# Row stages by single tiles: one 512-wide matmul for both token parts, and VectorE sums the halves

## The chip, the cores and the metric

The kernel runs on one core of a Trainium2 chip. Its metric is the device time of one execution in microseconds (us): the median of three runs before the change is 413.46 us. Five engines work side by side, each through its own queue in order: PE (TensorE) does matmuls, with the loads of its stationary operand shown apart as PEld; DVE (VectorE) and ACT (ScalarE) do elementwise work; POOL (GpSimd) does little here; SP (SyncE) issues the transfers. PE writes its results to PSUM, of which one accumulator tile here is 128 x 512 fp32, one bank; DVE and ACT read PSUM and work in SBUF.

## What is computed

One decoder layer of width 1024 on 256 tokens (two token tiles, t = 0 and 1) with a memory of 256 tokens. In the reference, cut short:

```python
h = rms_norm(x, g_pre_mix);  proj = h @ w_in        # MoBA attention and RetNet retention on proj
x = x + rms_norm(concat(mo, ro) @ w_out, g_post_mix)
q = rms_norm(x, g_pre_cross) @ w_cq                 # cross-attention, 4 heads of 256
k, v = split(rms_norm(mem, g_mem) @ w_ckv)
x = x + rms_norm(softmax(q k^T / 16) v @ w_co, g_post_cross)
gu = rms_norm(x, g_pre_ffn) @ w_gate_up             # d_ff = 2816 = 22 tiles of 128
x = x + rms_norm((silu(gu[:, :2816]) * gu[:, 2816:]) @ w_down, g_post_ffn)
```

All of it is fp32. The norms' row scales commute with the products: the kernel multiplies by the gain ahead of a matmul and by the inverse root mean square behind it.

## The kernel before, in words

**Three products for one.** Each fp32 operand is split in two parts of a faster format (fp32r): the high part is a rounded copy, the low part is what is left. A product is then three matmuls, high x high, high x low and low x high (helper `tri` and the loops of the three kinds of steps).

**Weights.** All weights lie in DRAM as 130 blocks of 128 x 1024 fp32 in the order of use. `load_weight` fetches a block (ring of 5 raw tiles), `split_weight` (L128 on) makes its two parts: the high one by ACT (L133), the low one by DVE (L134), in a ring of 9 tiles `hl`.

**Steps.** The whole program is a list of steps that is walked once, so PE's order is the list's. There are three kinds. A *col* step multiplies a token tile (stationary) by 512 weight columns (moving): six matmuls of 512 columns. A *down* step does the same for the last FFN product. A *row* step turns this round: the weights are stationary, 128 columns of them at a time, and the 256 tokens are moving, so that the result comes out transposed, as the next stage needs it. Row steps make the cross keys (k stage, `memT`), the cross queries (cq stage, `x1T`) and the gate and up products (`x2T`) apart from their first 512 columns.

A row block is 256 rows (two k tiles) by 512 columns (four tiles of 128 outputs). It feeds two steps, one for each pair of output tiles. A step is 12 matmuls of 256 columns: for two output tiles and two k tiles, high weights by high tokens (L868), the same weights by low tokens (L870), low weights by high tokens (L871). An accumulator holds the pair, 2 x 256 columns, and is finished after four blocks. Two accumulators are open at once.

**Stages.** In order: input projection (24 blocks, col), output projection (8, col), k (8, row), cq (8, row), cross values (8, col), cross output (8, col), first FFN chunk (8, col), then four gate/up stages (4 gate and 4 up blocks each, row) with a down stage (4 blocks) behind each, a last gate/up stage of two tiles (4 blocks) and the last 6 down blocks.

**Side work.** What DVE and ACT do besides the splits is written as generators. When a step finishes an accumulator, its `done` function does the work at once or spawns a generator; `yield n` lets it rest for n steps. The table `WAIT` holds these numbers by name. At the end of each step the due generators go on, then at most one weight block is split: if its ring place is free, if the pace allows it, and if no generator went on in this step or fewer than seven blocks are ahead (`low` 6). All engines follow the order in which this walk writes their instructions.

What becomes of a finished pair: `k_done` multiplies by the row of memory scales (`row_bcast`, DVE), copies the high part (ACT) and subtracts for the low part (DVE). `cq_done` splits straight from PSUM. `ffn_gate_T` multiplies by the row of scales (L511, DVE), takes Silu (L512, ACT), multiplies by the row again (L514, DVE). `ffn_up_T` multiplies the up accumulator by that (L520, DVE) and splits the product into `fT` (L524 ACT, L525 DVE), which the down steps read.

`post_and_pre` stands between stages: `post_add` adds the normed branch to x (L411), then ACT squares x for the next norm (L151), and after a wait `xw` PE transposes x; ACT and DVE scale it by the gains and split it into `x1T` or `x2T` (L427, L430), in two halves with a wait `xh` between them. The k stage is the time in which `x1T` is made; the cq stage reads it. `row_rms` makes the row of scales.

PSUM has four tiles of tag S (`accS`), three of tag B (`accB`) and one of tag C (`accC`).

Of the kernel before, what the change touches and what calls it, by code (L numbers as in the profile page):

```python
# [14 lines left out]
P = 128  # L15
# [7 lines left out]
NQ = 130  # L23

WAIT = {
# [7 lines left out]
}  # L33
WARM = 8

# [6 lines left out]
def tile_hybrid_layer(  # L42
# [127 lines left out]
    def row_rms(key):  # L170
# [3 lines left out]
        for t in range(2):  # L174
            nc.tensor.transpose(c[:, t, :], rstd[f"{key}{t}"][:, 0:1].to_broadcast([P, P]), ident)
        nc.scalar.activation(T[f"R_{key}"], c[:, 0:2, :].rearrange("p t k -> p (t k)"), AF.Copy)

    def row_bcast(key):
        return T[f"R_{key}"][:, None, :].to_broadcast([P, 2, 256])


    active = []
# [223 lines left out]
    def post_add(stage, t):  # L406
        ss, cg = posts.pop(f"{stage}{t}")
        r = inv_rms(f"p_{stage}{t}", ss[:, 0:1], ss[:, 1:2])
        for half in range(2):
            xs = x_sb[:, t, half * 512:(half + 1) * 512]  # L410
            nc.vector.scalar_tensor_tensor(xs, cg[half], r[:, 0:1], xs, op0=ALU.mult, op1=ALU.add)  # L411

    def post_and_pre(stage, t, g, dst_name, key):
        post_add(stage, t)
        ss = small(f"ssx_{stage}{t}")
        mean_square(ss[:, 0:1], x_sb[:, t, :], D)
        inv_rms(f"{key}{t}", ss[:, 0:1])
        yield WAIT[f"xw_{stage}{t}"]
        dst = T[dst_name]
        for half in range(2):  # L420
            a = accS(f"xt_{stage}{t}{half}")
            for j in range(4):
                k = half * 4 + j
                nc.tensor.transpose(a[:, j * P:(j + 1) * P], x_sb[:, t, k * P:(k + 1) * P], ident)
            for j in range(4):
                k = half * 4 + j
                nc.scalar.activation(dst[:, 0, k, tok(t)], a[:, j * P:(j + 1) * P], AF.Copy, scale=gp[:, g, k:k + 1])  # L427
            for j in range(4):
                k = half * 4 + j
                nc.vector.scalar_tensor_tensor(dst[:, 1, k, tok(t)], a[:, j * P:(j + 1) * P], gp[:, g, k:k + 1],  # L430
                                               dst[:, 0, k, tok(t)].bitcast(F32), op0=ALU.mult, op1=ALU.subtract)
                emitted.add((dst_name, k, t))
            if half == 0:
                yield WAIT[f"xh_{stage}{t}"]
        if stage == "cross" and t == 1:
            yield WAIT["xrow"]
            row_rms("x2")
# [66 lines left out]
        nc.scalar.activation(sg, acc, AF.Silu, scale=rstd[f"x2{t}"][:, 0:1])  # L504
        T[f"sg0_{t}"] = sg

    def ffn_gate_T(j, pair, acc):
        sg = tmp2k(f"sg{j}_{pair}")
        T[f"sg{j}_{pair}"] = sg
        s3 = sg.rearrange("p (j m) -> p j m", j=2)  # L510
        nc.vector.tensor_tensor(out=s3, in0=acc.rearrange("p (j m) -> p j m", j=2), in1=row_bcast("x2"), op=ALU.mult)  # L511
        nc.scalar.activation(sg, sg, AF.Silu)  # L512
        yield WAIT[f"sr{pair}"] if j < 5 else 0
        nc.vector.tensor_tensor(out=s3, in0=s3, in1=row_bcast("x2"), op=ALU.mult)  # L514
        emitted.add(f"sg{j}_{pair}")

    def ffn_up_T(j, pair, acc):
        need(f"sg{j}_{pair if j < 5 else 0}")
        f = tmp2k(f"f{j}_{pair}")
        nc.vector.tensor_tensor(out=f, in0=acc, in1=T[f"sg{j}_{pair}"], op=ALU.mult)  # L520
        k = 2 * pair if j < 5 else 0
        hi = T["fT"][:, j % 2, 0, k:k + 2, :].rearrange("p j m -> p (j m)")
        lo = T["fT"][:, j % 2, 1, k:k + 2, :].rearrange("p j m -> p (j m)")
        nc.scalar.activation(hi, f, AF.Copy)  # L524
        nc.vector.tensor_tensor(out=lo, in0=f, in1=hi.bitcast(F32), op=ALU.subtract)  # L525
        emitted.update(("fT", 4 * j + i, t) for i in (k, k + 1) for t in range(2))

    def final(t, half):
        nc.sync.dma_start(out[tok(t), half * 512:(half + 1) * 512], x_sb[:, t, half * 512:(half + 1) * 512])
# [30 lines left out]
            if t == 1:  # L560
                spawn(load_gpost(1, WAIT["gp1"]))

    def k_done(c, pair, acc):
        k = 4 * c + 2 * pair
        kf = tmp2k(f"kf{k}").rearrange("p (j m) -> p j m", j=2)
        nc.vector.tensor_tensor(out=kf, in0=acc.rearrange("p (j m) -> p j m", j=2), in1=row_bcast("mem"), op=ALU.mult)
        hi_lo(T["ckh"][:, k:k + 2, :], T["ckl"][:, k:k + 2, :], kf)

    def cq_done(c, pair, acc):
        k = 4 * c + 2 * pair  # L570
        hi_lo(T["cqh"][:, k:k + 2, :], T["cql"][c][:, 2 * pair:2 * pair + 2, :],
              acc.rearrange("p (j m) -> p j m", j=2))
        if k == 6:
            for t in range(2):
                spawn(cross_unit(t), WAIT[f"cu{t}"])

# [51 lines left out]
                continue  # L628
            steps.append(("col", base + i, t, st, kp, (c, t), s == 0, s + 1 == count[c], done))

    def row_steps(order, done, st):


        for c, kp in order:
            for pair in range(2):
                steps.append(("row", nq[0], pair, st, kp, (c, pair), kp == 0, kp == 3, done))
            nq[0] += 1

    def plain(chunks):
# [20 lines left out]
    for c in range(2):  # L660
        col_steps([(c, kp) for kp in (2, 3, 0, 1)], both, out_done, "mixT")
    mark("k")
    row_steps(plain([0, 1]), k_done, "memT")
    mark("cq")
    row_steps(plain([0, 1]), cq_done, "x1T")
    mark("v")
    col_steps(plain([0, 1]), both, v_done, "memT")
    mark("co")
# [6 lines left out]
        else:  # L675
            spawn(ffn_up(t, acc))

    def gu_done(c, pair, acc):
        j, up = c % 100, c >= 100
        if up:  # L680
            ffn_up_T(j, pair, acc)
        elif j == 5 and pair == 1:
            T["sg5_1"] = T["sg5_0"]
            ffn_up_T(j, pair, acc)
        else:
            spawn(ffn_gate_T(j, pair, acc))

    def down_steps(js, tiles):
        blocks = [(j, kk) for j in js for kk in range(4 if j < 5 else 2)]
# [6 lines left out]

    col_steps(plain([0, 1]), first_then, gu_first, "x2T")
    for j in range(1, 5):
        row_steps(plain([j]), gu_done, "x2T")
        row_steps(plain([100 + j]), gu_done, "x2T")  # L700
        if j < 4:
            down_steps([j - 1], both)
    down_steps([3], both)
    row_steps(plain([5]), gu_done, "x2T")
    down_steps([4, 5], [(0,)])
    blocks_base = nq[0] - 6
    for half in range(2):
# [100 lines left out]
    for i, s in enumerate(steps):  # L808
# [28 lines left out]
        elif s[0] == "col":  # L837
            _, q, t, st, kp, key, first, last, done = s
            if first:
                accs[key] = accB(f"acc{i}")  # L840
            acc = accs[key]
            h = hls[q].rearrange("p s (k n) -> p s k n", k=2)
            for kk in range(2):
# [8 lines left out]
                del accs[key]  # L852
                done(key[0], t, acc)
        elif s[0] == "row":
            _, q, pair, st, kp, key, first, last, done = s
            if first:
                accs[key] = accS(f"acc{i}") if st != "x2T" and key[0] == 1 else accB(f"acc{i}")
            acc = accs[key]
            h = hls[q].rearrange("p s (k n) -> p s k n", k=2)
            for b in range(2):  # L860
                dst = acc[:, b * 256:(b + 1) * 256]
                n = slice((2 * pair + b) * P, (2 * pair + b + 1) * P)
                for kk in range(2):
                    k = 2 * kp + kk
                    need((st, k, 0), (st, k, 1))
                    xh = T[st][:, 0, k, :]
                    xl = T[st][:, 1, k, :]
                    nc.tensor.matmul(dst, h[:, 0, kk, n], xh, start=(first and b == 0 and kk == 0), stop=False,  # L868
                                     skip_group_check=True)
                    nc.tensor.matmul(dst, h[:, 0, kk, n], xl, start=False, stop=False, skip_group_check=True)  # L870
                    nc.tensor.matmul(dst, h[:, 1, kk, n], xh, start=False, stop=(last and kk == 1),  # L871
                                     skip_group_check=True)
            if last:
                del accs[key]
                done(key[0], pair, acc)
        elif s[0] == "down":
            _, q, t, j, kk, halves = s
            for half in halves:
# [34 lines left out]
def _layout(inputs):  # L913
# [15 lines left out]
        blocks += cols(w_in, c * 512, k4)  # L929
    for c in range(2):  # L930
        blocks += cols(w_out, c * 512, (2, 3, 0, 1))
    w_cq, w_ckv, w_co = a["w_cq"][0], a["w_ckv"][0], a["w_co"][0]
    for w, cs in ((w_ckv, (0, 1)), (w_cq, (0, 1)), (w_ckv, (2, 3))):
        for c in cs:
            blocks += cols(w, c * 512, k4)
    for half in range(2):
        for c in range(2):
            blocks += cols(w_co, c * 512, (2 * half, 2 * half + 1))
# [3 lines left out]
    def down(j):  # L942
        return [dn[k * P:(k + 1) * P] for k in range(4 * j, min(4 * j + 4, ff // P))]

    for j in range(5):
        blocks += cols(gu, j * 512, k4) + cols(gu, ff + j * 512, k4)
        if 1 <= j < 4:
            blocks += down(j - 1)
    blocks += down(3)
    last = np.concatenate([gu[:, 2560:2816], gu[:, ff + 2560:ff + 2816]], axis=1)  # L950
    blocks += cols(last, 0, k4) + down(4) + down(5)
    weights = np.stack(blocks)

    def tiles_T(v):
# [54 lines left out]
```

## Time and profile before

| | us |
|---|---|
| median of three runs (413.32 to 413.69) | 413.46 |
| the profiled execution's own time | 413.18 |
| its span in the profile | 411.4 |
| DVE, splits of weights (L134, 132 operations) | 154.0 |
| ACT, splits of weights (L133, 132 operations) | 131.7 |
| gate/up stage (192 row matmuls), 275.44 to 298.48 | 23.04 |
| down stage (48 matmuls), 298.48 to 309.38 | 10.90 |

The profile is of one execution. Times of instructions are given from the span's start. Matmuls are pipelined: one is shown for longer than it holds PE up, and what it costs is the distance of its start to the next one's. Idle time of an engine stands with what ended it.

### The profile page before, as it was taken

How to read it: one execution, taken by the hardware profiler on the slowest of the kernel's cores; microseconds unless marked ns; L12 is line 12 of the kernel's file. 1: busy time of each engine (PE TensorE's matmuls, PEld its weight loads, DVE VectorE, ACT ScalarE, POOL GpSimd, SP SyncE). 2: the span in 40 equal slices, each digit the busy share in tenths (PEclk: the TensorE clock that was granted, in tenths of full speed). 3: DMA queues.
4: the chain of work that ended last, by engine and by line, in shares of the span. 5: the costliest groups of instructions: out<-in, count | busy, mean ns of one | idle time of the engine just before them, and what ended most of it. 6: DMA issues, size and time to landing. Idle time of an engine off the chain costs nothing.

```text
span 411.4 us, 6399 instructions
## 1 busy us (share of the span) xinstructions
PE 404.0 (98%) x2530; PEld 358.6 (87%) x2530; DVE 260.5 (63%) x356; ACT 219.0 (53%) x360; POOL 11.0 (3%) x21
## 2 busy tenths in 40 slices
PE   8999999999999999999999999999999999999994
PEld 4888787878899999888888899989989989998983
DVE  5876975866858884485367687664674764566332
ACT  5887686746656662584266666352453553444111
POOL 0010100000010000000011000000000000000000
PEclk9999999999999999999999999999999999999998
DMA  8998754475727674225414867676546447353001
GB/s 292 408 348 276 242 188 151 138 255 187 229 80 252 210 261 169 81 68 189 155 51 155 289 226 253 206 231 180 189 150 227 150 146 266 106 202 104 0 27 77
DMA packets 21630, 76.23 MB, mean 185 GB/s; under 512 B 2400, under 2 KB 2656, under 8 KB 21600
## 3 DMA queue, kind: packets, MB, share of 16 engines
q1 hardware_dynamic: 21456, 75.56, 54.3%
q8 instruction: 20, 0.33, 0.3%
q10 hardware_dynamic: 144, 0.26, 0.2%
q14 instruction: 10, 0.08, 0.1%
HBM read 74.76 MB, written 1.05 MB: 184 GB/s over the span
## 4 chain that ended last, share of the span: by engine, by line
PE 95%; issue 2%; DMA 1%; ACT 1%; DVE 0%; SPq 0%; DVEq 0%; POOLq 0%; POOL 0%
PE acc L871 12%; PE acc L868 12%; PE acc L870 12%; PE acc L848 12%; PE acc L850 12%; PE acc L849 12%; PE down L890 4%; PE down L892 4%; PE down L891 4%; PE acc L835 2%; DMA xr<-in_gx_dram 1%; PE s_m L276 1%; PE o_m L305 1%; PE pt_m L255 1%; PE ro L358 0%
## 5 line engine op out<-in xcount | busy, mean ns | idle before, releaser
L134 DVE TENSOR_TENSOR hl<-raw,hl 128x1024 fp32r<-128x1024 f32 (+1 forms) x132 | 154.0, 1197 | 49.6 <-ACT hl L133 49.4
L133 ACT ACTIVATE hl<-raw 128x1024 fp32r<-128x1024 f32 (+1 forms) x132 | 131.7, 1036 | 42.0 <-PE acc L871 15.0
L868 PE MATMUL acc<-x2T,hl 128*128 128x256 f32 x288 | 81.8, 284 | 0.0
L871 PE MATMUL acc<-x2T,hl 128*128 128x256 f32 x288 | 81.6, 283 | 0.0
L870 PE MATMUL acc<-x2T,hl 128*128 128x256 f32 x288 | 81.6, 283 | 0.0
L870 PEld LDWEIGHTS acc<-x2T,hl 128*128 128x128 f32 x288 | 55.3, 192 | 0.2
L868 PEld LDWEIGHTS acc<-x2T,hl 128*128 128x128 f32 x288 | 55.3, 192 | 0.2
L871 PEld LDWEIGHTS acc<-x2T,hl 128*128 128x128 f32 x288 | 55.3, 192 | 0.0
L890 PE MATMUL down<-hl,fT 128*128 128x512 f32 x88 | 34.3, 390 | 0.0
L891 PE MATMUL down<-hl,fT 128*128 128x512 f32 x88 | 34.3, 390 | 0.0
L892 PE MATMUL down<-hl,fT 128*128 128x512 f32 x88 | 34.3, 389 | 0.0
L848 PE MATMUL acc<-hl,xT 128*128 128x512 f32 x80 | 32.7, 409 | 0.0
L850 PE MATMUL acc<-hl,xT 128*128 128x512 f32 x80 | 31.3, 392 | 0.0
L849 PE MATMUL acc<-hl,xT 128*128 128x512 f32 x80 | 31.2, 390 | 0.0
L892 PEld LDWEIGHTS down<-hl,fT 128*128 128x128 f32 x88 | 16.5, 188 | 3.5
L890 PEld LDWEIGHTS down<-hl,fT 128*128 128x128 f32 x88 | 16.6, 188 | 3.3
L891 PEld LDWEIGHTS down<-hl,fT 128*128 128x128 f32 x88 | 16.6, 188 | 3.3
L512 ACT ACTIVATE sg<-sg 128x512 f32<-128x512 f32 x9 | 5.7, 632 | 24.9 <-DVE sg L511 24.9
L868 PE MATMUL acc<-memT,hl 128*128 128x256 f32 x64 | 18.4, 287 | 0.0
L870 PE MATMUL acc<-x1T,hl 128*128 128x256 f32 x64 | 18.1, 283 | 0.0
L871 PE MATMUL acc<-memT,hl 128*128 128x256 f32 x64 | 18.1, 283 | 0.0
L868 PE MATMUL acc<-x1T,hl 128*128 128x256 f32 x64 | 18.1, 283 | 0.0
(207 smaller groups left out, 727.8 us busy)
## 6 DMA issues: line engine op xcount, KB each, us to landing
raw<-in_weights_dram SPq DMA_DIRECT2D x129, 512.0 KB, 4.6
gpost<-in_gpost_dram SPq DMA_DIRECT2D x3, 512.0 KB, 6.0
x_sb<-in_x_dram SPq DMA_DIRECT2D x2, 512.0 KB, 6.9
memn<-in_mem_dram SPq DMA_DIRECT2D x2, 512.0 KB, 7.1
mr<-in_memT_dram SPq DMA_DIRECT2D x2, 512.0 KB, 5.2
out_dram<-x_sb SPq DMA_DIRECT2D x4, 256.0 KB, 2.0
xr<-in_gx_dram SPq DMA_DIRECT2D x1, 512.0 KB, 7.8
cst<-in_consts_dram SPq DMA_DIRECT2D x1, 512.0 KB, 8.6
```

The source lines that it names most:

```text
L133: nc.scalar.activation(h[:, 0, n], raw[:, n], AF.Copy)
L134: nc.vector.tensor_tensor(out=h[:, 1, n], in0=raw[:, n], in1=h[:, 0, n].bitcast(F32), op=ALU.subtract)
L835: nc.tensor.matmul(accs[(c, t)], T["xT"][:, hx, 2 * kp + kk, tok(t)], h[:, hw, :], start=begin, stop=False)
L848: nc.tensor.matmul(acc, xh, h[:, 0, kk, :], start=(first and kk == 0), stop=False)
L849: nc.tensor.matmul(acc, xh, h[:, 1, kk, :], start=False, stop=False)
L850: nc.tensor.matmul(acc, xl, h[:, 0, kk, :], start=False, stop=(last and kk == 1))
L868: nc.tensor.matmul(dst, h[:, 0, kk, n], xh, start=(first and b == 0 and kk == 0), stop=False, skip_group_check=True)
L870: nc.tensor.matmul(dst, h[:, 0, kk, n], xl, start=False, stop=False, skip_group_check=True)
L871: nc.tensor.matmul(dst, h[:, 1, kk, n], xh, start=False, stop=(last and kk == 1), skip_group_check=True)
L890: nc.tensor.matmul(acc, fh, wh, start=first, stop=False, skip_group_check=True)
L891: nc.tensor.matmul(acc, fh, wl, start=False, stop=False, skip_group_check=True)
L892: nc.tensor.matmul(acc, fl, wh, start=False, stop=last, skip_group_check=True)
```

## The change

The blocks of the row stages are cut otherwise. A block is now all eight k tiles of one output tile (8 x 128 columns), so one block makes one output tile, in two steps of four k tiles each. For each k tile two matmuls are issued: the high weights by both token parts, high and low, in one matmul of 512 columns, whose result fills both halves of the bank; and the low weights by the high token part, 256 columns, added to the first half. At the end the sum is first half plus second half: ACT copies the second half to SBUF, DVE adds the first from PSUM. The multiplications and splits behind it work on 256 columns, one tile at a time, and each is spawned as a generator with waits of its own. Gate and up tiles alternate. The order of the weight blocks in DRAM follows; the number of blocks stays 130.

```diff
-            _, q, pair, st, kp, key, first, last, done = s
...
-                for kk in range(2):
-                    k = 2 * kp + kk
-                    nc.tensor.matmul(dst, h[:, 0, kk, n], xh, ...)
-                    nc.tensor.matmul(dst, h[:, 0, kk, n], xl, ...)
-                    nc.tensor.matmul(dst, h[:, 1, kk, n], xh, ...)
+            _, q, half, st, nt, done = s
+            if half == 0:
+                accs["row"] = accB(f"acc{i}")
+            acc = accs["row"]
+            for k in range(4 * half, 4 * half + 4):
+                need((st, k, 0), (st, k, 1))
+                n = slice(k * P, (k + 1) * P)
+                nc.tensor.matmul(acc.rearrange("p (s m) -> p s m", s=2), hls[q][:, 0, n], T[st][:, :, k, :],
+                                 start=(k == 0), stop=False, skip_group_check=True)
+                nc.tensor.matmul(acc[:, 0:256], hls[q][:, 1, n], T[st][:, 0, k, :], start=False, stop=(k == 7),
+                                 skip_group_check=True)
+            if half == 1:
+                spawn(done(nt, acc))
...
+    def ffn_gate_T(i, acc):
+        buf = tmp2k(f"sg{i}")
+        T[f"sg{i}"] = buf
+        sg = buf[:, 0:256]
+        nc.scalar.activation(sg, acc[:, 256:512], AF.Copy)
+        yield WAIT["g_add"]
+        nc.vector.tensor_tensor(out=sg, in0=acc[:, 0:256], in1=sg, op=ALU.add)
+        nc.vector.tensor_tensor(out=sg, in0=sg, in1=T["R_x2"], op=ALU.mult)
+        yield WAIT["g_silu"]
         nc.scalar.activation(sg, sg, AF.Silu)
+        yield WAIT["g_row"]
+        nc.vector.tensor_tensor(out=sg, in0=sg, in1=T["R_x2"], op=ALU.mult)
+    def ffn_up_T(i, acc):
+        buf = T.pop(f"sg{i}")
+        f = buf[:, 256:512]
+        nc.scalar.activation(f, acc[:, 256:512], AF.Copy)
+        yield WAIT["u_add"]
+        nc.vector.tensor_tensor(out=f, in0=acc[:, 0:256], in1=f, op=ALU.add)
+        nc.vector.tensor_tensor(out=f, in0=f, in1=buf[:, 0:256], op=ALU.mult)
+        yield WAIT["u_hl"]
+        hi_lo(T["fT"][:, (i // 4) % 2, 0, i % 4, :], T["fT"][:, (i // 4) % 2, 1, i % 4, :], f)
...
+    def k_done(i, acc):
+        kf = tmp2k(f"kf{i}")[:, 0:256]
+        nc.scalar.activation(kf, acc[:, 256:512], AF.Copy)
+        yield WAIT["k_add"]
+        nc.vector.tensor_tensor(out=kf, in0=acc[:, 0:256], in1=kf, op=ALU.add)
+        nc.vector.tensor_tensor(out=kf, in0=kf, in1=T["R_mem"], op=ALU.mult)
+        yield WAIT["k_hl"]
+        hi_lo(T["ckh"][:, i, :], T["ckl"][:, i, :], kf)
...
     def post_and_pre(stage, t, g, dst_name, key):
         post_add(stage, t)
+        yield WAIT[f"xa_{stage}{t}"]
...
-                accs[key] = accB(f"acc{i}")
+                accs[key] = accC(f"acc{i}").rearrange("p j k -> p (j k)") if st == "memT" and key == (1, 0) else accB(f"acc{i}")
```

`cq_done` is cut to one tile in the same way as `k_done`, without the multiplication. New waits: g_add, u_add, k_add and q_hl 0, g_silu and g_row 1, u_hl and k_hl 2; xa_mix0 3, xa_mix1 5, xa_cross 2 each. Changed ones: xw_mix0 4 to 2, xw_mix1 9 to 5, xw_cross0 7 to 5, xw_cross1 3 to 2, xrow 1 to 3, nm_c1 3 to 5, cpv0 6 to 7. In DRAM, a gate/up stage's blocks are gate tile, up tile, gate tile, and so on.

More of the change, by code (lines that the diff above doesn't have):

```diff
@@ L176, in row_rms @@
         nc.scalar.activation(T[f"R_{key}"], c[:, 0:2, :].rearrange("p t k -> p (t k)"), AF.Copy)
-    def row_bcast(key):
-        return T[f"R_{key}"][:, None, :].to_broadcast([P, 2, 256])
     active = []
@@ L505, in ffn_gate @@
         T[f"sg0_{t}"] = sg
[L507 to L526, printed above, removed]
+    def ffn_gate_T(i, acc):
[7 more added lines that the diff above has]
+        yield WAIT["g_silu"]
+        nc.scalar.activation(sg, sg, AF.Silu)
+        yield WAIT["g_row"]
+        nc.vector.tensor_tensor(out=sg, in0=sg, in1=T["R_x2"], op=ALU.mult)
+        emitted.add(f"sg{i}")
+    def ffn_up_T(i, acc):
[3 more added lines that the diff above has]
+        yield WAIT["u_add"]
+        need(f"sg{i}")
+        nc.vector.tensor_tensor(out=f, in0=acc[:, 0:256], in1=f, op=ALU.add)
+        nc.vector.tensor_tensor(out=f, in0=f, in1=buf[:, 0:256], op=ALU.mult)
+        yield WAIT["u_hl"]
+        hi_lo(T["fT"][:, (i // 4) % 2, 0, i % 4, :], T["fT"][:, (i // 4) % 2, 1, i % 4, :], f)
+        emitted.update(("fT", i, t) for t in range(2))
     def final(t, half):
@@ L561, in out_done, with cq_done @@
                 spawn(load_gpost(1, WAIT["gp1"]))
[L563 to L573, printed above, removed]
+    def k_done(i, acc):
[6 more added lines that the diff above has]
+        hi_lo(T["ckh"][:, i, :], T["ckl"][:, i, :], kf)
+    def cq_done(i, acc):
+        qf = tmp2k(f"qf{i}")[:, 0:256]
+        nc.scalar.activation(qf, acc[:, 256:512], AF.Copy)
+        yield WAIT["k_add"]
+        nc.vector.tensor_tensor(out=qf, in0=acc[:, 0:256], in1=qf, op=ALU.add)
+        yield WAIT["k_hl"] if i < 7 else WAIT["q_hl"]
+        hi_lo(T["cqh"][:, i, :], T["cql"][i // 4][:, i % 4, :], qf)
+        emitted.add(f"cq{i}")
+        if i == 7:
+            need(*[f"cq{k}" for k in range(8)])
             for t in range(2):
@@ L629, in col_steps, with row_steps @@
             steps.append(("col", base + i, t, st, kp, (c, t), s == 0, s + 1 == count[c], done))
[L631 to L636, printed above, removed]
+    def row_steps(tiles, done, st):
+        for i in tiles:
+            for half in range(2):
+                steps.append(("row", nq[0], half, st, i, done))
             nq[0] += 1
@@ L662, in tile_hybrid_layer @@
     mark("k")
-    row_steps(plain([0, 1]), k_done, "memT")
+    row_steps(range(8), k_done, "memT")
     mark("cq")
-    row_steps(plain([0, 1]), cq_done, "x1T")
+    row_steps(range(8), cq_done, "x1T")
     mark("v")
@@ L676, in gu_first, with gu_done, gu_steps @@
             spawn(ffn_up(t, acc))
[L678 to L686, printed above, removed]
+    def gu_done(i, acc):
+        return ffn_up_T(i - 100, acc) if i >= 100 else ffn_gate_T(i, acc)
+    def gu_steps(tiles):
+        row_steps([i + up for i in tiles for up in (0, 100)], gu_done, "x2T")
     def down_steps(js, tiles):
@@ L698, in tile_hybrid_layer @@
     for j in range(1, 5):
-        row_steps(plain([j]), gu_done, "x2T")
-        row_steps(plain([100 + j]), gu_done, "x2T")
+        gu_steps(range(4 * j, 4 * j + 4))
         if j < 4:
@@ L703, in tile_hybrid_layer @@
     down_steps([3], both)
-    row_steps(plain([5]), gu_done, "x2T")
+    gu_steps((20, 21))
     down_steps([4, 5], [(0,)])
@@ L854, in tile_hybrid_layer @@
         elif s[0] == "row":
-            _, q, pair, st, kp, key, first, last, done = s
[L856 to L862, printed above, removed]
-                for kk in range(2):
-                    k = 2 * kp + kk
[L865 to L875, printed above, removed]
+            _, q, half, st, nt, done = s
[11 more added lines that the diff above has]
+                spawn(done(nt, acc))
         elif s[0] == "down":
@@ L931, in _layout, with rows @@
         blocks += cols(w_out, c * 512, (2, 3, 0, 1))
+    def rows(w, i):
+        return [w[:, i * P:(i + 1) * P].reshape(8, P, P).transpose(1, 0, 2).reshape(P, D)]
     w_cq, w_ckv, w_co = a["w_cq"][0], a["w_ckv"][0], a["w_co"][0]
-    for w, cs in ((w_ckv, (0, 1)), (w_cq, (0, 1)), (w_ckv, (2, 3))):
-        for c in cs:
-            blocks += cols(w, c * 512, k4)
+    for w in (w_ckv, w_cq):
+        for i in range(8):
+            blocks += rows(w, i)
+    for c in (2, 3):
+        blocks += cols(w_ckv, c * 512, k4)
     for half in range(2):
@@ L943, in down, with gate_up @@
         return [dn[k * P:(k + 1) * P] for k in range(4 * j, min(4 * j + 4, ff // P))]
-    for j in range(5):
-        blocks += cols(gu, j * 512, k4) + cols(gu, ff + j * 512, k4)
-        if 1 <= j < 4:
+    def gate_up(tiles):
+        return [b for i in tiles for b in rows(gu, i) + rows(gu, ff // P + i)]
+    blocks += cols(gu, 0, k4) + cols(gu, ff, k4)
+    for j in range(1, 5):
+        blocks += gate_up(range(4 * j, 4 * j + 4))
+        if j < 4:
             blocks += down(j - 1)
-    blocks += down(3)
-    last = np.concatenate([gu[:, 2560:2816], gu[:, ff + 2560:ff + 2816]], axis=1)
-    blocks += cols(last, 0, k4) + down(4) + down(5)
+    blocks += down(3) + gate_up((20, 21)) + down(4) + down(5)
     weights = np.stack(blocks)
```

15 rows, old and new, of the table WAIT are left out of this document.

## The prediction

> **What bounds the kernel now.** I read the busy times of the page first, then its chain of work that ended last, then the waits of PE:
>
> ```profile
> PE 404.0 (98%) x2530; PEld 358.6 (87%) x2530; DVE 260.5 (63%) x356; ACT 219.0 (53%) x360; POOL 11.0 (3%) x21
> ...
> PE 95%; issue 2%; DMA 1%; ACT 1%; DVE 0%; SPq 0%; DVEq 0%; POOLq 0%; POOL 0%
> ```
>
> ```profile
> PE warm L723 <- DVE junk L716: 1.2, 1, 1.2
> ```
>
> PE is busy for 404.0 of the span of 411.4 us, the chain is 95% PE, and PE's waits have one entry, 1.2 us ahead of the warm-up. So after the opening PE never waits for another engine, and the time is the sum of PE's pitches (start of one matmul to start of the next). An edit counts if it changes that sum, or if it makes PE wait. DVE and ACT have room on the mean, not necessarily in each stage.
>
> The change touches the row stages. Their lines, one by one:
>
> ```profile
> L868 PE MATMUL acc<-x2T,hl x288: 277/283/364, 240.6 to 388.4; 128*128 128x256 f32 x144
> ...
> L868 PE MATMUL acc<-memT,hl x64: 278/283/365, 111.8 to 136.3; 128*128 128x256 f32 x64
> ...
> L868 PE MATMUL acc<-x1T,hl x64: 283/283/284, 136.6 to 159.3; 128*128 128x256 f32 x64
> ```
>
> That is 288+64+64 = 416 executions of L868, and the loop issues L870 and L871 once behind each: 1248 matmuls of 256 columns. Their duration of 283 ns is not their cost, since they overlap. The cost is the pitch, which the timeline gives. First and last of 36 rows in a gate/up stage, then of 33 rows in a down stage, both PE alone:
>
> ```profile
> 249.77 0.28 PE L868 MATMUL acc<-x2T,hl 128*128 128x256 f32 x1
> ...
> 253.97 0.28 PE L871 MATMUL acc<-x2T,hl 128*128 128x256 f32 x1
> ```
>
> ```profile
> 265.70 0.39 PE L892 MATMUL down<-hl,fT 128*128 128x512 f32 x1
> ...
> 272.95 0.39 PE L891 MATMUL down<-hl,fT 128*128 128x512 f32 x1
> ```
>
> 35 pitches in 4.20 us are 0.1200 us for 256 columns; 32 pitches in 7.25 us are 0.2266 us for 512. So 256 more columns cost 0.1066 us, and each matmul costs 0.0134 us beyond its columns (0.1200 - 0.1066). Row stages take 1248 x 0.1200 = 149.8 us of the span.
>
> **The change part by part.**
>
> *Matmuls.* For each of the 416 pairs (tile of 128 outputs, k tile) three matmuls of 256 columns become one of 512 (high weights on both token parts) and one of 256 (low weights). The columns stay at 768; one fixed cost goes. Before: 3 x 0.1200 = 0.3600 us. After: 0.2266 + 0.1200 = 0.3466 us. 416 x 0.0134 = 5.6 us less.
>
> The trace has no stage in which widths alternate. The nearest rows are those where one stage hands over to the other:
>
> ```profile
> 264.41 0.28 PE L871 MATMUL acc<-x2T,hl 128*128 128x256 f32 x1
> 264.53 0.40 PE L890 MATMUL down<-hl,fT 128*128 128x512 f32 x1
> 264.77 0.40 PE L891 MATMUL down<-hl,fT 128*128 128x512 f32 x1
> 265.00 0.39 PE L892 MATMUL down<-hl,fT 128*128 128x512 f32 x1
> ```
>
> ```profile
> 275.22 0.39 PE L892 MATMUL down<-hl,fT 128*128 128x512 f32 x1
> 275.44 0.28 PE L868 MATMUL acc<-x2T,hl 128*128 128x256 f32 x1
> 275.56 0.28 PE L870 MATMUL acc<-x2T,hl 128*128 128x256 f32 x1
> 275.67 0.28 PE L871 MATMUL acc<-x2T,hl 128*128 128x256 f32 x1
> ```
>
> The first 512 behind a 256 took 0.24 us, the next 0.23; the first 256 behind a 512 took 0.12, the next 0.11. An alternating pair therefore lies between 0.23 + 0.11 = 0.34 us (saving 8.3 us in all) and 0.24 + 0.12 = 0.36 us (saving nothing). I take 0.3466: it lies between, and comes from two long stretches, where the resolution of 0.01 us does not matter. The moving operand is now two runs of 256 columns instead of one; no row shows such a one, and its bounds are the same: at best one 512, at worst two 256 (pair 0.36).
>
> *Weights.* A block now holds one tile's 128 columns for all eight k tiles. There are still 130 blocks of the same size, each split once, and each feeds two steps as before, so loads and splits keep their count. A step is four pairs, 1.39 us, where it was twelve matmuls, 1.44 us.
>
> *Evacuation.* The rows that price it, the 256-wide operations by their nearest kin:
>
> ```profile
> L134 DVE TENSOR_TENSOR hl<-raw,hl 128x1024 fp32r<-128x1024 f32 x126 | 150.2, 1221 | 48.9 <-ACT hl L133 48.8
> ...
> L511 DVE TENSOR_TENSOR sg<-acc,R_x 128x512 f32<-128x512 f32 x9 | 6.2, 692 | 14.4 <-PE acc L871 14.4
> ...
> L347 DVE TENSOR_TENSOR ra<-rs,cst 128x256 f32<-128x256 f32 x2 | 0.8, 418 | 0.0
> ```
>
> ```profile
> L133 ACT ACTIVATE hl<-raw 128x1024 fp32r<-128x1024 f32 x126 | 128.2, 1056 | 41.0 <-PE acc L871 15.0 <-PE down L892 13.3 <-issue 6.7
> ...
> L512 ACT ACTIVATE sg<-sg 128x512 f32<-128x512 f32 x9 | 5.7, 632 | 24.9 <-DVE sg L511 24.9
> ...
> L328 ACT ACTIVATE kr<-c_r 128x256 f32<-128x256 f32 x2 | 0.8, 396 | 0.0
> ```
>
> A gate/up stage (four gate and four up tiles, eight blocks) had eight DVE operations of 512, 8 x 0.692 = 5.5 us. It gets 3 of 256 for each of eight tiles, 24 x 0.418 = 10.0 us. With eight splits, 9.8 us, that is 19.8 us of DVE in a stage of 64 x 0.3466 = 22.2 us: 89%. ACT goes from four operations of 512 (2.5 us) to sixteen of 256 (16 x 0.396 = 6.3 us), with its splits (8.4 us) 14.8 of 22.2 us. Both still fit. The next stage is a relief, as the windows of one gate/up and one down stage show (columns: length, PE, PEld, DVE, ACT, POOL, clock, DMA share, GB/s):
>
> ```profile
> 111.84:136.62 24.78, 24.78 (x210) 24.77 (x209) 17.88 (x36) 15.29 (x32) 2.22 (x4) 1.00 0.53 174
> ...
> 275.44:298.48 23.04, 23.04 (x194) 23.04 (x193) 11.67 (x12) 8.87 (x10) 0.00 (x0) 1.00 0.63 198
> 298.48:309.38 10.90, 10.90 (x50) 9.02 (x49) 7.93 (x8) 5.71 (x7) 0.00 (x0) 1.00 0.47 163
> ```
>
> The three accumulator buffers let DVE trail PE by two tiles, 5.5 us, and a split is forced when six blocks or fewer are ahead, so one late operation stops nothing. I cost the extra evacuation at 0. If the cover is gone, it costs what the last rival below says.
>
> *The k stage* is the narrowest, the first window above: DVE 17.88 of 24.78 us. Four operations of 512 in it go and seven tiles bring 21 of 256: 17.88 - 4 x 0.692 + 21 x 0.418 = 23.9 us, in a stage 0.9 us shorter (64 x 0.0134), 23.9 us. DVE is full there, and x1T is made in the same stage, which the first query tile now needs whole (all k tiles in its two steps) instead of two k tiles per block. In the trace of before, DVE's last part of x1T (the second token tile's k tiles 4 to 7) and the query stage stand so:
>
> ```profile
> 133.55 1.12 DVE L430 SCALAR_TENSOR_TENSOR x1T<-xt_mix,xg,x1T 128x128 fp32r<-128x128 f32 x4
> 134.59 1.22 DVE L134 TENSOR_TENSOR hl<-raw,hl 128x1024 fp32r<-128x1024 f32 x1
> 135.72 1.12 DVE L430 SCALAR_TENSOR_TENSOR x1T<-xt_mix,xg,x1T 128x128 fp32r<-128x128 f32 x4
> ```
>
> It ends at 136.84; the query stage began at 136.62 and asked for these k tiles two blocks later. Now they are asked for one step into a stage that starts 0.9 us earlier, at 136.62 - 0.9 + 1.39 = 137.1. Left in its place, it is ready 0.3 us before that. The waits move it one step on (half 1 at xa 5 + xw 5 + xh 3 = 13 steps behind the post step; before 9 + 3 = 12), but xa now lets a tile's evacuation into DVE's and ACT's queues ahead of the squares of x1, where before both engines stood waiting for one another. So PE waits there between 0 and, with DVE a whole k tile late, about 3 us, once. I take 0, because counting DVE's k stage operations in the new order, with the six splits that the ring calls for, puts the end of x1T at about 134 to 135 us.
>
> *Other moves.* The row of x2's scales is made two steps later (xrow 3), with some ten steps of column work left ahead of its first reader, the first gate tile. The second token tile's cross softmax is transposed two steps later, and the first value product one step later, still ahead of the co step that reads it; one value accumulator takes the spare bank. The last up tile (21) is read five down blocks, 5 x 6 x 0.2266 = 6.8 us, behind its last matmul; its chain is two ACT and three DVE operations of 256, 2 x 0.396 + 3 x 0.418 = 2.0 us, and two steps of waiting, 2 x 6 x 0.2266 = 2.7 us. All 0. The ending is untouched.
>
> *Sum.* 5.6 us off and nothing on. The profiled execution took 413.18 us, span 411.4, and stands 0.28 us below the median of the three runs, 413.46. From the median: 407.9, rounded to 408.0.
>
> **The rivals.**
>
> *x1T is late* (or another short wait of PE of 2 to 4 us in all): 409.9 to 411.9. For it: the full k stage. Against it: the count above.
>
> *The fixed cost does not go* (pair 0.36, by the handover rows or the two runs): 413.5, the same. Against it: two long stretches agree on one line only if a matmul, not a column, carries 0.0134 us. The Trainium skill's page TensorE: Matmul & The Clock Gate, section Back-to-back issue gap, gives a warm matmul its columns at 2.4 GHz plus 2.5 ns; by that the change would save 416 x 2.5 ns = 1.0 us and end at 412.4. This trace has 13.4 ns in that place, with the clock at 1.00 in the windows above, so I keep the row.
>
> *More goes* (pair 0.34): 413.46 - 8.3 = 405.2. For it: the 0.23 and 0.11 us behind a handover. Against it: they are two rows, and on the same edges 0.24 and 0.12.
>
> *DVE takes over in the gate/up stages, slower.* DVE does its operations in order, so a wait for a tile stops the splits behind it. The waits of DVE in before:
>
> ```profile
> DVE sg L511 <- PE acc L871: 14.4, 9, 4.8
> DVE f L520 <- PE acc L871: 7.5, 4, 2.0
> ...
> DVE fT L525 <- ACT fT L524: 6.3, 9, 0.7
> ```
>
> 28.2 us over nine gate and nine up evacuations are 6.3 us for the four of a stage. If they stayed beside the 19.8 us, a stage would need 26.1 us of DVE against 22.2 of PE: 3.9 us more for each of 4.5 stages, 17.6 us, and 413.5 - 5.6 + 17.6 = 425.5. It decides once PE's waits reach 5.6 us in all, 1.2 us for a stage. Against it: these waits are those of an engine that is ahead of PE; one that trails does not wait for PE, and the down stage (DVE 7.93 of 10.90 us, half of it splits) gives back what a stage lost.
>
> **How the numbers follow.** Forecast (406.5 to 409.5) 0.66; x1T late 0.14; more goes 0.06; nothing goes 0.07; DVE takes over 0.07. The three that save give faster 0.86, the others same 0.07 and slower 0.07; 0.2% is 0.8 us, about what runs of this kernel can tell. The range 405.9 to 411.9 holds the first two, 8 in 10; its ends are a pair of 0.342 us and PE waits of 4 us.
>
> **What would show it.** In the changed profile: PE's row stages with 832 matmuls, the pair at 0.347 us in the timeline (0.36 refutes the first step), gate/up stages 22.2 us long and down stages still 10.9; no wait of PE on x1T at the start of the query stage (one of over 1 us makes it the first rival); DVE near 20 us in a gate/up window without PE waiting on an accumulator or a split (if PE does, the last rival). The prediction is wrong if the span falls by less than 2 us or more than 7.5.

## The result, and the profile after

The changed kernel takes 410.39 us (median of 4 runs, 409.71 to 410.97), the kernel before 413.57 us (4 runs, 413.32 to 413.74). The ratio is 0.9923, 95% interval 0.9906 to 0.994: faster by 3.2 us, where the prediction had 408.0 and so 5.5 us. The sign is right, the time lies in the stated range, and the gain lies where it was put, in PE's pitches. The size of the main term is not right.

The page after, busy times and chain, then the waits of PE:

```profile
PE 401.5 (98%) x2114; PEld 337.2 (82%) x2114; DVE 283.6 (69%) x456; ACT 238.4 (58%) x438; POOL 11.9 (3%) x21
...
PE 96%; issue 2%; ACT 0%; DVE 0%; DVEq 0%; POOLq 0%; POOL 0%
```

```profile
PE warm L730 <- DVE junk L723: 1.2, 1, 1.2
```

PE has 416 matmuls fewer and still waits for nothing after the opening. DVE is busy for 23 us more and ACT for 19 us more, all of it beside PE. So the whole difference is again in PE's pitches. The windows are those of the k, query, gate/up and down stages, each from its first matmul to the next stage's first:

```profile
112.42:136.63 24.21, 24.21 (x145) 21.34 (x144) 22.18 (x51) 18.05 (x42) 2.21 (x4) 1.00 0.55 181
136.63:159.24 22.61, 22.61 (x130) 19.60 (x129) 17.55 (x29) 13.51 (x25) 0.00 (x0) 1.00 0.67 205
274.38:296.98 22.60, 22.60 (x130) 19.62 (x128) 14.64 (x26) 10.20 (x20) 0.00 (x0) 1.00 0.55 187
296.98:307.88 10.90, 10.90 (x50) 9.01 (x49) 9.37 (x11) 7.37 (x9) 0.00 (x0) 1.00 0.76 234
```

The query stage of before, which the prediction does not show, was this:

```profile
136.62:159.65 23.03, 23.03 (x194) 23.03 (x193) 16.41 (x18) 11.51 (x14) 0.00 (x0) 1.00 0.74 251
```

A gate/up stage is 22.60 us long instead of 23.04, not 22.2. The down stage is 10.90 as it was. The query stage went from 23.03 to 22.61 us, and the k stage lost 0.57 us of its 24.78. A pair of matmuls thus takes 22.60/64 = 0.3531 us. The timeline inside that stage shows it at work, thirteen rows, of which the first six and the last stand here:

```profile
279.67 0.40 PE L869 MATMUL acc<-x2T,hl 128*128 128x512 f32 x1
279.90 0.28 PE L871 MATMUL acc<-x2T,hl 128*128 128x256 f32 x1
280.01 0.40 PE L869 MATMUL acc<-x2T,hl 128*128 128x512 f32 x1
280.25 0.28 PE L871 MATMUL acc<-x2T,hl 128*128 128x256 f32 x1
280.37 0.40 PE L869 MATMUL acc<-x2T,hl 128*128 128x512 f32 x1
280.61 0.28 PE L871 MATMUL acc<-x2T,hl 128*128 128x256 f32 x1
...
281.79 0.40 PE L869 MATMUL acc<-x2T,hl 128*128 128x512 f32 x1
```

Six pairs in 281.79 - 279.67 = 2.12 us, 0.3533 each. The 512-wide matmul takes 0.23 to 0.24 us where a long stretch of its kind had 0.2266; the 256-wide one takes 0.11 to 0.12. Over 416 pairs: 416 x (0.3600 - 0.3533) = 2.8 us. That is most of the gain. The profiled execution took 410.63 us against 413.18 (span 408.9 against 411.4), although its opening was half a microsecond longer: from the k stage's first matmul to the end it took 296.5 us against 299.6, 3.1 us less. Of the 0.3 us beyond the pairs, 0.23 us lie in the column steps between the query and the first gate/up stage (80.99 to 80.76 us), whose matmuls are the same.

### The profile page after: what moved, and what is told of

It is laid out like the page before. It is cut to its first block, busy times and chain, and to the rows that moved or that the text cites. A ratio compares the mean times of both kernels' runs of the same rounds, so it can differ in the third digit from the quotient of the medians.

```text
span 408.9 us, 5752 instructions
## 1 busy us (share of the span) xinstructions
PE 401.5 (98%) x2114; PEld 337.2 (82%) x2114; DVE 283.6 (69%) x456; ACT 238.4 (58%) x438; POOL 11.9 (3%) x21
## 4 chain that ended last, share of the span: by engine, by line
PE 96%; issue 2%; ACT 0%; DVE 0%; DVEq 0%; POOLq 0%; POOL 0%
PE acc L869 24%; PE acc L871 12%; PE acc L855 12%; PE acc L856 12%; PE acc L857 12%; PE down L889 4%; PE down L890 4%; PE down L891 4%; PE acc L842 3%; PE warm L730 1%; PE s_m L274 1%; PE o_m L303 1%; PE pt_m L253 1%; PE ro L356 0%; PE co L443 0%
## 5 line engine op out<-in xcount | busy, mean ns | idle before, releaser
L869 PE MATMUL acc<-x2T,hl 128*128 128x512 f32 x288 | 102.2, 399 | 0.0
L871 PE MATMUL acc<-x2T,hl 128*128 128x256 f32 x288 | 80.9, 281 | 0.0
L869 PEld LDWEIGHTS acc<-x2T,hl 128*128 128x128 f32 x288 | 54.1, 188 | 13.3
L871 PEld LDWEIGHTS acc<-x2T,hl 128*128 128x128 f32 x288 | 54.4, 189 | 0.2
L869 PE MATMUL acc<-memT,hl 128*128 128x512 f32 x64 | 22.9, 400 | 0.0
L869 PE MATMUL acc<-x1T,hl 128*128 128x512 f32 x64 | 22.7, 399 | 0.0
L515 ACT ACTIVATE sg<-sg 128x256 f32<-128x256 f32 x18 | 7.5, 417 | 21.1 <-DVE sg L513 21.1
L510 ACT ACTIVATE sg<-acc 128x256 f32<-128x256 f32 x18 | 6.8, 377 | 20.8 <-PE acc L871 20.4
L871 PE MATMUL acc<-x1T,hl 128*128 128x256 f32 x64 | 18.0, 281 | 0.0
L871 PE MATMUL acc<-memT,hl 128*128 128x256 f32 x64 | 18.0, 281 | 0.0
L857 PEld LDWEIGHTS acc<-hl,xT 128*128 128x128 f32 x80 | 15.0, 188 | 3.3
```

Source lines behind the costliest of these rows:

```text
L857: nc.tensor.matmul(acc, xl, h[:, 0, kk, :], start=False, stop=(last and kk == 1))
L869: nc.tensor.matmul(acc.rearrange("p (s m) -> p s m", s=2), hls[q][:, 0, n], T[st][:, :, k, :], start=(k == 0), stop=False, skip_group_chec ...
L871: nc.tensor.matmul(acc[:, 0:256], hls[q][:, 1, n], T[st][:, 0, k, :], start=False, stop=(k == 7), skip_group_check=True)
```

## The experiments

**What the evacuation costs, and what the matmul's form brings.** One part of the change undone: the wide matmul back in two.

```diff
-                nc.tensor.matmul(acc.rearrange("p (s m) -> p s m", s=2), hls[q][:, 0, n], T[st][:, :, k, :],
-                                 start=(k == 0), ...)
+                nc.tensor.matmul(acc[:, 0:256], hls[q][:, 0, n], T[st][:, 0, k, :], start=(k == 0), ...)
+                nc.tensor.matmul(acc[:, 256:512], hls[q][:, 0, n], T[st][:, 1, k, :], start=False, ...)
```

> The changed kernel with its 512-wide matmul cut back into two of 256 columns with the same high weights; blocks, evacuation and waits stay those of the change. In the changed trace a pair costs 0.3533 us in place of 0.3600. If only PE's pitches differ (evacuation and the new waits cost nothing), 416 x 0.0067 = 2.8 us come back: 413.2 us, like the kernel before, and no wait of PE. If the evacuation or the waits eat part of the gain (rival), it is slower than the kernel before by what they eat: 413.5 + 2.5 = 416.

Measured: 413.61 us, ratio to the kernel before 0.9998 (0.9989 to 1.0007). Its gate/up window:

```profile
275.49:298.52 23.03, 23.03 (x194) 23.03 (x192) 14.17 (x26) 10.51 (x20) 0.00 (x0) 1.00 0.56 181
```

The stage is 23.03 us long, 0.3598 a pair, as before the change. With three times as many evacuation operations on DVE and four times as many on ACT, each of half the width, and with all the new waits in place, the time is that of the kernel before to 0.1%. The evacuation is hidden, and the wide matmul is the gain, but for about 0.2 us: the column steps behind the query stage are as short in this run as in the change (159.93 to 240.68, 80.75 us).

**Two runs of columns, or the change of width.** The token parts side by side:

```diff
-        T[name] = stp.tile([P, 2, 8, 256], F32R, tag=tag, name=name)
+        T[name] = stp.tile([P, 8, 2, 256], F32R, tag=tag, name=name).rearrange("p k s m -> p s k m")
```

> The changed kernel with the token parts laid side by side for each k tile, so that the 512-wide matmul reads one run of 512 columns and not two runs of 256. Theory A (the missing 0.0067 us of a pair comes from the change of width at every matmul): nothing changes, pair 0.353, 410.4 us. Theory B (it comes from the two runs): pair 0.3466, 416 x 0.0067 = 2.8 us less, 407.6 us.

Measured: 410.71 us, ratio 0.993 (0.9918 to 0.9942), and the same stage length:

```profile
273.80:296.40 22.60, 22.60 (x129) 19.59 (x128) 14.29 (x26) 10.20 (x20) 0.00 (x0) 1.00 0.58 185
```

One run of 512 or two of 256 is the same to PE here. Theory B falls.

**No change of width at all.** The low weights over both token parts too; this adds low x low to the sum:

```diff
-                nc.tensor.matmul(acc[:, 0:256], hls[q][:, 1, n], T[st][:, 0, k, :], start=False, stop=(k == 7), ...)
+                nc.tensor.matmul(acc.rearrange("p (s m) -> p s m", s=2), hls[q][:, 1, n], T[st][:, :, k, :],
+                                 start=False, stop=(k == 7), ...)
```

> The changed kernel with the low weights also run over both token parts, 512 columns (it adds the product of both low parts to the second half of the bank, which the reference's fp32 product contains too): every matmul of a row stage is 512 wide with two runs, and the width never changes there. Theory A: 0.2267 a matmul, pair 0.4533, 416 x 0.1000 = 41.6 us more: 452.0 us. Theory B: the two runs cost 0.0067 in each of two matmuls, pair 0.4667, 457.5 us.

Measured: 452.55 us, as theory A had it.

```profile
293.59:322.61 29.02, 29.02 (x130) 24.03 (x128) 14.51 (x26) 11.30 (x20) 0.00 (x0) 1.00 0.41 132
```

29.02/128 = 0.2267 us a matmul, with two runs of columns and the weights stationary; the down stage of before had 0.2266 with one run and the tokens stationary. High and low weights alternate here as in the change, so it is not their alternation that costs.

**Sorted by width.** The same matmuls in another order: high x 4, low x 4, then low x 4, high x 4, so that runs of one width are eight long.

```diff
-            for k in range(4 * half, 4 * half + 4):
...
+            ks = range(4 * half, 4 * half + 4)
+            for low in ((0, 1), (1, 0))[half]:
+                for k in ks:
...
+                    if low == 0:
+                        nc.tensor.matmul(acc.rearrange("p (s m) -> p s m", s=2), hls[q][:, 0, n], T[st][:, :, k, :], ...)
+                    else:
+                        nc.tensor.matmul(acc[:, 0:256], hls[q][:, 1, n], T[st][:, 0, k, :], ...)
```

> The changed kernel with the matmuls of a step sorted by width: first half step four high then four low, second half step four low then four high, so the width changes once in a step and not at every matmul. Theory A (width changes cost): eight pairs have one round trip in place of eight; a round trip between long stretches costs about 0.018 us in the handover rows, so a pair is 0.3466 + 0.018/8 = 0.349 us and 1.8 us are saved: 408.6 us. Theory B (two runs): pair stays 0.353, 410.4 us.

Measured: 408.83 us, ratio 0.9888 (0.9876 to 0.9901), against 0.993 (0.9918 to 0.9942) for the alternating order on the same chip (the run above with the token parts side by side).

```profile
273.59:295.93 22.34, 22.34 (x129) 19.66 (x128) 14.56 (x26) 10.02 (x19) 0.00 (x0) 1.00 0.56 190
```

22.34/64 = 0.3491 us a pair, the expected 0.349. Theory A holds: a matmul's pitch depends on the widths just ahead of it.

**Other lengths of run.** Three more orders: a tile's eight high matmuls in one step and its eight low ones in the other, in turns (runs of 16); high, high, low, low (runs of 2); and high x 4, low x 4 (runs of 4). Of each edit only the loop's line is shown, with a remark behind it.

```diff
+            for low in ((q + half) % 2,):                                        # runs of 16, k in range(8)
+            for low, ks in ((0, ks[:2]), (1, ks[:2]), (0, ks[2:]), (1, ks[2:])):  # runs of 2
+            for low in (0, 1):                                                    # runs of 4
```

> As the sorted kernel of before this one, with longer runs of one width: a tile's eight high matmuls in one step and its eight low ones in the other, in turns by tile, so the width changes once in a tile. The sorted kernel's trace has 0.3491 us a pair and so 8 x (0.3491 - 0.3467) = 0.0196 us a round trip of widths. Theory A: one round trip for 16 pairs, 0.3467 + 0.0196/16 = 0.3479 us, 416 x 0.0012 = 0.5 us less than 408.8: 408.3 us. Rival: the first step of a tile now needs all eight k tiles, and steps are of unequal length (1.81 and 0.96 us), so PE comes to wait on x1T, on an accumulator or a split: over 409 us, with a wait of PE in its trace.

> As the changed kernel with runs of two (high, high, low, low): half as many changes of width as in the change. If each position behind a change of width has its price, as in the sorted kernel's trace (512: 0.234, 0.236; 256: 0.113, 0.119), a pair is 0.702/2 = 0.351 us, 416 x 0.0023 = 1.0 us less than the change: 409.6 us. If a round trip has one fixed price of 0.0196 us whatever the run's length, a pair is 0.3467 + 0.0098 = 0.3565 us: 411.9 us.

> As the changed kernel with runs of four (four high, four low in each half step). Runs of two cost 0.0032 us a round trip of widths, runs of eight 0.019. If the price grows with the run's length as the pitches behind a change of width in the sorted kernel do (512: 0.234, 0.236, 0.228, 0.232; 256: 0.113, 0.119, 0.120, 0.120), a round trip costs 0.015 us and a pair is 0.3467 + 0.015/4 = 0.3505 us, a gate/up stage 22.43 us. If only runs of one are dear and a short run costs 0.0032 us whatever its length, a pair is 0.3475 us and the stage 22.24 us.

Measured: runs of 16 408.83 us (ratio 0.9877, 0.9862 to 0.9891), runs of 2 408.97 us (0.9882, 0.9865 to 0.9898), runs of 4 409.35 us in a single run. Their gate/up windows in that order:

```profile
273.98:296.24 22.26, 22.26 (x129) 19.68 (x128) 14.91 (x27) 10.35 (x20) 0.00 (x0) 1.00 0.60 196
```

```profile
273.66:295.95 22.29, 22.29 (x130) 19.45 (x129) 14.43 (x26) 10.01 (x19) 0.00 (x0) 1.00 0.59 192
```

```profile
273.63:296.06 22.43, 22.43 (x130) 19.62 (x129) 14.30 (x26) 10.12 (x20) 0.00 (x0) 1.00 0.58 186
```

| run of one width | us a pair (stage/64) | above 0.3467, for one round trip of widths |
|---|---|---|
| 1 (the change) | 0.3531 | 0.0064 |
| 2 | 0.3483 | 0.0032 |
| 4 | 0.3505 | 0.015 |
| 8 | 0.3491 | 0.019 |
| 16 | 0.3478 | 0.018 |

From four on, a round trip costs 0.015 to 0.019 us, as the pitches behind a change of width add up to, and longer runs spread it over more pairs; the prices by position had 0.3505 for runs of four and it is 0.3505. That agreement is of the sum: the first 256 behind a 512 takes 0.117 us on the mean there, against 0.113 in the sorted kernel. Runs of two were expected at 0.351 or 0.3565 and have 0.3483: both expectations missed. Runs of one have 0.3531, where the first prices alone (0.234 + 0.113) would make 0.347. So the pitch depends on more than the position behind the last change, and a price list by position is no law for short runs. The runs of 16 were expected 0.5 us below the runs of eight; the stage is 0.08 us shorter as expected. The medians are equal, 408.83 both, but they come from two chips on which the kernel before took 413.98 and 413.60 us, so against it the runs of 16 save 5.1 us and the runs of eight 4.8, within each other's interval. After the opening PE waited for nothing in it.

**How much cover is left.** The sorted kernel with one or two more VectorE operations for each gate and up tile, into a scratch tile that nothing reads:

```diff
         nc.vector.tensor_tensor(out=sg, in0=acc[:, 0:256], in1=sg, op=ALU.add)
+        for _ in range(2):                                   # in the second run: range(1)
+            nc.vector.tensor_tensor(out=scr, in0=sg, in1=T["R_x2"], op=ALU.mult)
```

(the same behind the sum of an up tile)

> The sorted kernel with two more VectorE multiplications of 128 x 256 for each gate and each up tile, into a scratch tile that nothing reads. It asks how much cover the extra evacuation has. A gate/up and a down stage take 33.2 us and hold 24.0 us of VectorE in the changed trace; 16 x 0.418 = 6.7 us more are 30.7 us. If VectorE only has to fit over both stages: no wait of PE, 408.8 us. If it has to fit within the gate/up stage with its waits for PE and ACT (14.6 + 6.7 us and 5 us of waits in 22.3 us): PE waits about 4 us in each of 4.5 stages, 427 us.

> The sorted kernel with one more VectorE multiplication of 128 x 256 for each gate and each up tile into the scratch tile, half of what the run before added. That one made PE wait 2.0 us in each full gate/up stage and 3.8 us in the last down stage. If the price is linear from the first added operation (VectorE already full): half of it, about 414 us. If there is cover that the second operation used up: no wait of PE, 408.8 us.

Measured: two more, 419.17 us (ratio 1.0128, 1.0109 to 1.0147); one more, 409.26 us (0.988, 0.9864 to 0.9897), as without. PE's waits with two more (three shorter ones lie in the opening), and the gate/up windows with two and with one:

```profile
PE acc L877 <- DVE sg L529: 3.9, 3, 1.3
PE down L898 <- ACT fT L447: 1.9, 1, 1.9
```

```profile
275.13:299.47 24.34, 22.92 (x130) 19.50 (x128) 20.48 (x36) 12.71 (x22) 0.00 (x0) 1.00 0.63 212
```

```profile
274.02:296.36 22.34, 22.34 (x129) 19.67 (x128) 18.57 (x32) 11.68 (x21) 0.00 (x0) 1.00 0.65 217
```

With one more DVE is busy 18.57 of 22.34 us and PE does not notice. With two more it is busy 20.48 of 24.34 us, 84%, and PE waits on accumulators that DVE has not read yet. Yet DVE was not full. PE went on at 293.37 us, when DVE had read the accumulator (L529, from 292.90 on); shortly before, DVE and ACT had waited for each other:

```profile
290.02 0.42 ACT L518 ACTIVATE sg<-sg 128x256 f32<-128x256 f32 x1 [2.49 <-DVE sg L516]
290.35 1.04 ACT L135 ACTIVATE hl<-raw 128x1024 fp32r<-128x1024 f32 x1
```

```profile
291.42 1.22 DVE L136 TENSOR_TENSOR hl<-raw,hl 128x1024 fp32r<-128x1024 f32 x1 [1.43 <-ACT hl L135]
292.56 0.42 DVE L520 TENSOR_TENSOR sg<-sg,R_x 128x256 f32<-128x256 f32 x1
292.90 0.42 DVE L529 TENSOR_TENSOR sg<-acc,sg 128x256 f32<-128x256 f32 x1
```

ACT waited 2.49 us for DVE's multiplication ahead of its Silu, then copied a weight's high part, and DVE sat idle for 1.43 us until it had that part. With three accumulators DVE can trail by two tiles only, and these waits are part of the trail; what each part is worth is not shown. The busy share alone does not tell: in the changed kernel's k stage DVE is busy for 22.18 of 24.21 us, 92%, and PE waits for nothing.

Both expectations of the run with two more missed: it was neither free nor 4 us a stage (427 us). Three gate/up stages are 2.0 us longer than in the sorted kernel, the first 0.7 us, and the last down stage 3.8 us. In that one PE waits 1.9 us, and 1.3 us behind the wait its matmuls of 512 columns come 0.43 us apart in place of 0.23. The granted clock (the column behind POOL) is 0.50 there, and the next matmuls have 0.23 us again:

```profile
402.17:405.15 2.98, 2.98 (x8) 2.30 (x7) 2.16 (x4) 1.04 (x4) 0.55 (x1) 0.50 0.00 0
```

## Why the prediction was right and where it was wrong

*PE's pitches bound the kernel.* Right. After the opening every time here is the pitches' sum, and PE waits only where VectorE got two operations too many.

*The matmul term.* This is the step that failed: "After: 0.2266 + 0.1200 = 0.3466 us. 416 x 0.0134 = 5.6 us less." The pair takes 0.3531 to 0.3533 us, inside the bounds that the handover rows gave (0.34 to 0.36), and saves 2.8 us. I took pitches from two stretches of one width for an order in which the width changes at every matmul. That the two stretches "agree on one line" was no evidence for it: two points lie on a line in any case. The mechanism, one fixed cost a matmul, is right: without changes of width 512 columns cost 0.2267 us (expected 0.2267), in long runs a pair comes to 0.3478, and then nearly all of the 5.6 us is there (413.98 to 408.83 us, 5.1 us). Half of the gain went into the order. By the first handover pair in the prediction, 0.24 + 0.12, it would have been nothing, so the answer lay between the values that I had, and the value that I took from the long stretches was too favourable. That the stated range held 410.39 us was in part luck: the time lies outside the forecast's own 406.5 to 409.5 and in the band that was given to a late x1T (409.9 to 411.9), and x1T was not late.

*The two runs of columns.* I gave them the same bounds. They cost nothing: one run or two, 22.60 us.

*The evacuation at 0.* Right, shown by the undone matmul: 0.9998. The operations cost 0.418 to 0.425 us as priced by the one row of its kind. For a gate/up stage I counted 19.8 us of DVE; it has 14.64, and the down stage behind it 9.37, so 24.0 against 19.8 + 4.9 = 24.7. Six splits lie in the first window and seven in the second, where I had counted eight and four: part of the splits slips into the down stage, as the last rival's answer had it.

*x1T.* DVE's last part of it, after:

```profile
131.35 1.22 DVE L135 TENSOR_TENSOR hl<-raw,hl 128x1024 fp32r<-128x1024 f32 x1
...
133.76 1.12 DVE L429 SCALAR_TENSOR_TENSOR x1T<-xt_mix,xg,x1T 128x128 fp32r<-128x128 f32 x4
```

It ends at 134.88, "about 134 to 135" in the prediction. The query stage began at 136.63 without a wait. DVE is busy for 22.18 of the 24.21 us of the k stage, where I had counted 23.9.

*The rivals.* "The fixed cost does not go" was the nearest in size: half of it did not. By the 2.5 ns that the Trainium skill's page TensorE: Matmul & The Clock Gate gives for an isolated matmul in its section Back-to-back issue gap, the change would, by estimate, have saved 1.0 us, and no order could have saved 5. The measured 0.2267 and 0.1200 us decide for 13.4 ns in this kernel, where every matmul has a weight load of its own (2114 of each); whether the load is the reason is not shown. VectorE did not take over; in the sorted kernel it held PE up once it had two more operations for a tile.

*What stays open.* Why the change of width costs, and why runs of two are cheaper than runs of four, is not shown: the trace has starts and modelled ends, not what PE waits for inside. Also left: the profiled execution after reached the first transposes of q at 29.1 us, before at 28.5, on the same opening code; the traces of the kernels above, all with this opening, have 28.5 to 29.8, so a single comparison can be off by half a microsecond or more through the opening alone.

## What to carry to other kernels

Where PE never waits, count pitches, not columns: a matmul less is a fixed cost less, here 13.4 ns, as long as the order keeps one width for a while. Price an order from a stretch that has that order, or put the matmuls so that they form long stretches; sorting the same instructions by width took 0.26 us off a gate/up stage (22.60 to 22.34), 1.7 us over the 416 pairs. Hidden work stays hidden only as far as the accumulators let an engine trail, its waits for other engines included, and a kernel with one and one with two more operations for a tile tell how far off the edge is.

## What the runs showed of the hardware that was not expected

A 256-wide fp32r matmul takes 0.1200 us and a 512-wide one 0.2267 us in stretches of their own, but in strict alternation the two take 0.3531 us together, 6.4 ns more than their sum. In runs of two they take 0.3483 us, in runs of four 0.3505. The two 256-column halves of a moving operand may lie apart at no cost (22.60 us a stage either way). A single wait of PE of 1.9 us was followed by 3.0 us and more at a granted clock of 0.50, in which a 512-wide matmul took 0.43 us.
